# Matmul diagonal with softmax: reading half of the partitions in another block order

## The chip, the core and the metric

The kernel runs on one core of a Trainium2 chip. The metric is the device time of one execution in microseconds (us). Four of the core's engines have work here: VectorE (DVE in the profile) multiplies and sums, ScalarE (ACT) copies, sums some rows and takes exponentials, SyncE (SP) issues nearly all transfers, and sixteen DMA engines move the data between HBM and SBUF, the on-chip memory of 128 partitions. TensorE is not used.

## What is computed

```python
B, N, D = 8, 4096, 512          # x, y: float32
gram = np.matmul(x, y.transpose(0, 2, 1))
diag = np.diagonal(gram, axis1=1, axis2=2)
diag = diag - diag.max(axis=-1, keepdims=True)
exp = np.exp(diag)
return (exp / exp.sum(axis=-1, keepdims=True)).astype(np.float32)
```

Only the diagonal of the product is wanted, so each output needs one dot product of a row of x with the same row of y: 8 x 4096 dot products of length 512, then a softmax over the 4096 values of each batch. Each input has 67.1 MB and is read once; the output has 0.13 MB.

## The kernel before

**Tiling.** The eight batches are two sets of four (`Q`). In a set, a batch has 32 partitions (`G`), and each partition has 128 consecutive rows (`C`) of the batch, that is 128 x 512 x 4 B = 256 KB one after the other in HBM. Partition p of a set thus begins 256 KB behind partition p - 1, over all 128 partitions. A step `t` takes 32 of the 128 rows (`R`) of every partition: 64 KB a partition from x and 64 KB from y. There are eight steps (`S`): 0 to 3 for the first set, 4 to 7 for the second. `columns(t, r0, n)` gives the place of a step's rows among the 128, and with it the columns of `diag[set]` (128 partitions x 128) that receive the dot products.

**Buffers.** There are two tiles for x (`xs`, steps alternate) and one for y (`ys`). `xflat` and `yflat` are the same memory seen as 128 x 16384 elements (and some more).

**A step of the loop (lines 132 to 143).** SyncE issues one load of x (L70, helper `load_x`) and one of y (L73, `load_y`), 8 MB each, in this order over all steps. ScalarE copies the last 6 rows of y to `side` (L135). VectorE multiplies x by y in place, 26 rows from `ys` and 6 rows from `side` (L77), so that `ys` is free after the first of the two. It then sums 30 rows (L80), and ScalarE sums the other 2 (L85). The load of y for step t + 1 has to wait until the first product of step t has read `ys`; the load of x for step t + 2 has to wait until the sums of step t have read their tile. The x of step t + 1 has been issued before that, so it is what the queue works on during the products of step t.

**Softmax of the first set.** After step 3 `exps` takes the maximum of `diag[0]` along the columns (L105), then over the 32 partitions of a batch (L99), and the exponential with its sum (L112). `normalize` (L116 to L119) follows in step 4 and leaves the result in `res[0]`. It is not stored at once.

**The end.** Step 6 has other shares between VectorE and ScalarE. Step 7 is loaded in eleven pieces (lines 163 to 184) and worked off row by row with a fused multiply and sum (L88). Behind the last load, the one of L184, SyncE issues the stores of `res[0]` (L191) in six pieces: four of 16 partitions and two of 32. Then the softmax of the second set runs, and ScalarE issues the store of `res[1]` (L193).

**Order and waits of transfers.** Everything SyncE issues goes through one queue in the order of the program. A transfer signals its end on one of eight semaphores, which are taken in turn; a transfer whose semaphore is still in use by the one eight places earlier waits for that one.

Of the kernel before, what the change touches and what calls it, by code (L numbers as in the profile page):

```python
# [11 lines left out]
def kernel(  # L12
# [6 lines left out]
    nc = tc.nc  # L19
# [5 lines left out]
    B, N, D = x.shape  # L25
    P = nc.NUM_PARTITIONS
    G = 32
    Q = P // G
    C = N // G
    R = 32  # L30
    H = R // 2
# [10 lines left out]
    xv = x.rearrange("(s b) (j c) d -> s (b j) c d", b=Q, j=G)  # L42
    yv = y.rearrange("(s b) (j c) d -> s (b j) c d", b=Q, j=G)
    ov = out.rearrange("(s b) (j c) -> s (b j) c", b=Q, j=G)
# [5 lines left out]
    xflat = [big.tile([P, R * D + E], f32, name=f"xs{i}") for i in range(2)]  # L50
    yflat = big.tile([P, R * D + E], f32, name="ys")
    xs = [t[:, : R * D].rearrange("p (r d) -> p r d", d=D) for t in xflat]
    ys = yflat[:, : R * D].rearrange("p (r d) -> p r d", d=D)
# [3 lines left out]
    res = [small.tile([P, C], f32, name=f"res{i}") for i in range(B // Q)]  # L57

    def columns(t, r0, n):
        c0 = t % (C // R) * R + r0  # L60
        return slice(c0, c0 + n)

    def rows(t, r0, n):
        return xs[t % 2][:, r0 : r0 + n, :]

    def dots_of(t, r0, n):
        return diag[t * R // C][:, columns(t, r0, n)]

    def load_x(t, r0, n):
        nc.sync.dma_start(out=rows(t, r0, n), in_=xv[t * R // C, :, columns(t, r0, n), :])  # L70

    def load_y(t, r0, n):
        nc.sync.dma_start(out=ys[:, r0 : r0 + n, :], in_=yv[t * R // C, :, columns(t, r0, n), :])  # L73

    def products(t, r0, n, yt):
        xt = rows(t, r0, n)
# [30 lines left out]
    def exps(i, d):  # L107
        mxp = small.tile([P, 1], f32, name=f"mxp{i}")
        largest(mxp, d)
        nmx = over_quadrant(f"nmx{i}", mxp, Alu.max, negate=True)  # L110
        sump = small.tile([P, 1], f32, name=f"sump{i}")
        nc.scalar.activation(out=res[i], in_=diag[i][:, :C], func=Act.Exp, bias=nmx, scale=1.0, accum_out=sump)  # L112
        return sump

    def normalize(i, sump):
        total = over_quadrant(f"sum{i}", sump, Alu.add)  # L116
        rc = small.tile([P, 1], f32, name=f"rc{i}")
        nc.vector.reciprocal(out=rc, in_=total)  # L118
        nc.vector.tensor_single_scalar(out=res[i], in_=res[i], scalar=rc, op=Alu.mult)  # L119
# [12 lines left out]
    for t in range(S - 2):  # L132
        load_x(t, 0, R)
        load_y(t, 0, R)
        nc.scalar.activation(out=side, in_=ys[:, R - K :, :], func=Act.Copy)  # L135
        if t == C // R:
            normalize(0, sump)
        products(t, 0, R - K, ys[:, : R - K, :])
        products(t, R - K, K, side)
        sums(t, 0, R - W)  # L140
        sums_act(t, R - W, W)
        if t == C // R - 1:
            sump = exps(0, diag[0])

    t = S - 2
    load_x(t, 0, R)
    load_y(t, 0, R)
    spare = rows(t + 1, R - L, L)
    nc.scalar.activation(out=spare, in_=ys[:, F - L : F, :], func=Act.Copy)  # L149
# [13 lines left out]
    for load, n in (  # L163
        (load_x, H - 1), (load_y, F), (load_x, 8), (load_y, 9), (load_x, 6), (load_y, 3), (load_y, 1)
    ):
        load(t, upto[load], n)
        upto[load] += n
        both = min(upto.values())
        dots(t, done, both - done)
        done = both  # L170
        if done == F:
            largest(diag[1][:, C : C + 1], diag[1][:, C - 2 * R : C - R + H])

    first = (R - 3) * D
# [12 lines left out]
    met = small.tile([P, C - R], f32, name="met")  # L187
    nc.scalar.activation(out=met, in_=diag[1][:, : C - R], func=Act.Copy)  # L188

    for p, n in ((0, H), (H, H), (2 * H, H), (3 * H, H), (4 * H, 2 * H), (6 * H, 2 * H)):  # L190
        nc.sync.dma_start(out=ov[0, p : p + n, :], in_=res[0][p : p + n, :])  # L191
    normalize(1, exps(1, diag[1][:, C - R + H :]))
    nc.scalar.dma_start(out=ov[1], in_=res[1])  # L193

# [29 lines left out]
```

## Time and profile before

| | |
|---|---|
| median of 3 runs | 320.05 us (319.78 to 320.19) |
| the profiled execution | 319.75 us |
| its span, first to last instruction | 318.0 us |
| VectorE busy | 241.7 us (76%) |
| ScalarE busy | 49.9 us (16%) |
| read from HBM, mean rate over the span | 134.22 MB, 423 GB/s |
| y of step 0 lands | 42.15 us |
| last piece of x lands | 313.20 us |

The page shows one profiled execution. Engine rows give the busy time, the share of the span and the number of instructions. The DMA digits show, in 40 equal slices, the mean busy share of the 16 DMA engines in tenths, with 9 for 90% or more. A DMA packet is the piece of a transfer that one DMA engine moves at a time; here a packet of a big load is one partition's 64 KB. The chain of waits goes back from the last instruction to what released it, step by step, so it shows which work set the end. "SPq" is SyncE's queue, "ACTq" that of ScalarE.

### The profile page before, as it was taken

How to read it: one execution, taken by the hardware profiler on the slowest of the kernel's cores; microseconds unless marked ns; L12 is line 12 of the kernel's file. 1: busy time of each engine (PE TensorE's matmuls, PEld its weight loads, DVE VectorE, ACT ScalarE, POOL GpSimd, SP SyncE). 2: the span in 40 equal slices, each digit the busy share in tenths (PEclk: the TensorE clock that was granted, in tenths of full speed). 3: DMA queues.
4: the chain of work that ended last, by engine and by line, in shares of the span. 5: the costliest groups of instructions: out<-in, count | busy, mean ns of one | idle time of the engine just before them, and what ended most of it. 6: DMA issues, size and time to landing. Idle time of an engine off the chain costs nothing.

```text
span 318.0 us, 320 instructions
## 1 busy us (share of the span) xinstructions
DVE 241.7 (76%) x101; ACT 49.9 (16%) x97; POOL 0.2 (0%) x4
## 2 busy tenths in 40 slices
DVE  0000069995899939999399995999939998599995
ACT  1000030100301003010020103101030100596700
POOL 0000000000000000000000000000000000000000
DMA  9999999999999999999999999999999999999993
GB/s 381 412 396 486 437 396 437 478 404 396 486 437 396 445 478 396 396 486 437 396 470 453 396 396 511 412 396 478 445 396 412 495 412 396 433 439 404 442 410 131
DMA packets 3970, 134.37 MB, mean 423 GB/s; under 512 B 512, under 2 KB 896, under 8 KB 1536
## 3 DMA queue, kind: packets, MB, share of 16 engines
q1 hardware_dynamic: 3824, 134.29, 97.9%
q10 hardware_dynamic: 144, 0.07, 0.1%
q14 instruction: 2, 0.02, 0.0%
HBM read 134.22 MB, written 0.13 MB: 423 GB/s over the span
## 4 chain that ended last, share of the span: by engine, by line
DMA 70%; DVE 28%; issue 0%; SPq 0%; ACT 0%; DVEq 0%
DMA ys<-in_y_dram 59%; DVE xs L77 28%; DMA xs<-in_x_dram 11%; DVE xs L88 0%; SPq L73 0%; SPq L70 0%; DVE res L119 0%; DVE sum L99 0%; DVE nmx L99 0%; ACT res L112 0%; DVE mxp L105 0%; DVE rc L118 0%; DVEq L77 0%; DVEq L88 0%; SPq L130 0%
## 5 line engine op out<-in xcount | busy, mean ns | idle before, releaser
L77 DVE TENSOR_TENSOR xs<-xs,ys 128x13312 f32<-128x13312 f32 (+2 forms) x8 | 96.7, 12091 | 69.9 <-DMA ys<-in_y_dram 69.9
L80 DVE TENSOR_REDUCE diag<-xs 128x30 f32<-128x15360 f32 (+1 forms) x7 | 98.1, 14019 | 0.2
L85 ACT ACTIVATE xs<-xs 128x512 f32<-128x512 f32 x42 | 25.9, 618 | 90.4 <-DVE xs L77 90.4
L135 ACT ACTIVATE side<-ys 128x3072 f32<-128x3072 f32 x6 | 16.6, 2765 | 124.0 <-DMA ys<-in_y_dram 124.0
L88 DVE SCALAR_TENSOR_TENSOR xs<-xs,ys 128x512 f32<-128x512 f32 (+2 forms) x33 | 20.0, 673 | 0.8 <-DMA ys<-in_y_dram 0.7
L77 DVE TENSOR_TENSOR xs<-xs,side 128x3072 f32<-128x3072 f32 x6 | 20.1, 3351 | 0.0
L85 ACT ACTIVATION_READ_ACCUMULATOR xs<-xs 128x1 f32 x42 | 7.9, 188 | 0.0
L149 ACT ACTIVATE xs<-ys 128x4608 f32<-128x4608 f32 x1 | 4.0, 4045 | 19.9 <-DMA ys<-in_y_dram 19.9
L112 ACT ACTIVATE res<-diag,nmx 128x128 f32<-128x128 f32 x2 | 0.8, 403 | 29.8 <-DVE nmx L99 29.8
L77 DVE TENSOR_TENSOR xs<-xs,xs 128x4608 f32<-128x4608 f32 x1 | 5.0, 4951 | 0.0
L88 DVE DVE_READ_ACCUMULATOR xs<-xs,ys 128x1 f32 x33 | 2.8, 84 | 0.0
L123 ACT ACT_TABLE_LOAD x1 | 1.3, 1283 | 0.7 <-PEq L208 0.7
L99 DVE TRANSPOSE_TENSOR_REDUCE sum<-sump 128x1 f32<-128x32 f32 x2 | 0.4, 211 | 1.2 <-ACT res L112 1.2
L127 DVE MEMSET ys<- 128x1 f32 x1 | 0.1, 59 | 1.4 <-PEq L208 1.4
L119 DVE TENSOR_SCALAR res<-res,rc 128x128 f32<-128x128 f32 x2 | 0.6, 286 | 0.1
L105 DVE TENSOR_REDUCE mxp<-diag 128x1 f32<-128x128 f32 (+1 forms) x2 | 0.5, 228 | 0.1
L99 DVE TRANSPOSE_TENSOR_REDUCE nmx<-mxp 128x1 f32<-128x32 f32 x2 | 0.4, 211 | 0.1
L105 DVE TENSOR_REDUCE diag<-diag 128x1 f32<-128x64 f32 (+1 forms) x2 | 0.4, 204 | 0.0
L118 DVE RECIPROCAL rc<-sum 128x1 f32<-128x1 f32 x2 | 0.3, 162 | 0.1
L112 ACT ACTIVATION_READ_ACCUMULATOR res<-diag,nmx 128x1 f32 x2 | 0.4, 188 | 0.0
L188 ACT ACTIVATE met<-diag 128x96 f32<-128x96 f32 x1 | 0.3, 284 | 0.0
L208 POOL MEMSET const-bfloat16-1.0<- 128x1 bf16 x1 | 0.1, 101 | 0.0
(3 smaller groups left out, 0.3 us busy)
## 6 DMA issues: line engine op xcount, KB each, us to landing
ys<-in_y_dram SPq DMA_DIRECT2D x1, 4352.0 KB, 14.8
xs<-in_x_dram SPq DMA_DIRECT2D x1, 3840.0 KB, 14.1
ys<-in_y_dram SPq DMA_DIRECT2D x1, 2304.0 KB, 12.2
xs<-in_x_dram SPq DMA_DIRECT2D x1, 2048.0 KB, 19.3
xs<-in_x_dram SPq DMA_DIRECT2D x1, 1536.0 KB, 15.6
ys<-in_y_dram SPq DMA_DIRECT2D x1, 768.0 KB, 16.9
ys<-in_y_dram SPq DMA_DIRECT2D x3, 256.0 KB, 18.2
xs<-in_x_dram SPq DMA_DIRECT2D x1, 608.0 KB, 18.1
```

What stands on the lines that cost most here:

```text
L77: nc.vector.tensor_tensor(out=xt, in0=xt, in1=yt, op=Alu.mult)
L80: nc.vector.tensor_reduce(out=dots_of(t, r0, n), in_=rows(t, r0, n), axis=X, op=Alu.add)
L85: nc.scalar.activation(out=row, in_=row, func=Act.Copy, accum_out=dots_of(t, r, 1))
L88: nc.vector.scalar_tensor_tensor(out=xt, in0=xt, scalar=1.0, in1=yt, op0=Alu.mult, op1=Alu.mult, accum_out=out)
L99: nc.vector.tensor_reduce(out=got, in_=column.to_broadcast([P, G]), axis=X, op=op, negate=negate, apply_transpose=True)
L105: nc.vector.tensor_reduce(out=out, in_=d, axis=X, op=Alu.max)
L112: nc.scalar.activation(out=res[i], in_=diag[i][:, :C], func=Act.Exp, bias=nmx, scale=1.0, accum_out=sump)
L118: nc.vector.reciprocal(out=rc, in_=total)
L119: nc.vector.tensor_single_scalar(out=res[i], in_=res[i], scalar=rc, op=Alu.mult)
L123: nc.scalar.preload_act_table(Act.Exp)
L135: nc.scalar.activation(out=side, in_=ys[:, R - K :, :], func=Act.Copy)
L149: nc.scalar.activation(out=spare, in_=ys[:, F - L : F, :], func=Act.Copy)
```

## The change

The loads of steps 0 to 3 get a new source. For partitions 0 to 63 it is block t of 32 rows as before; for partitions 64 to 127 it is block t ^ 2, so 2, 3, 0, 1 over the four steps. Both halves are still one transfer: its source is a pattern written out by hand that counts 2 halves, then 64 partitions, then the 64 KB. The destination is the flat view of the tile, 128 partitions by 64 KB. From step 4 on the source is what it was, written flat.

The columns of `diag[0]` stay those of step t for all partitions, so in partitions 64 to 127 the columns 0 to 63 and 64 to 127 have changed places. The store of the first set puts this right: it goes in eight pieces of 16 partitions, and each row is stored as two halves of 64 elements (256 B), which are exchanged where p is 64 or more.

```diff
+    def source(a, t, r0, n):
+        if t >= C // R:
+            return (xv if a is x else yv)[t * R // C, :, columns(t, r0, n), :].rearrange("p c d -> p (c d)")
+        lower, upper = t * R * D, (t ^ 2) * R * D
+        return bass.AP(
+            a.tensor, lower + r0 * D, [[Q // 2 * N * D + upper - lower, 2], [C * D, P // 2], [1, n * D]]
+        )
+
     def load_x(t, r0, n):
-        nc.sync.dma_start(out=rows(t, r0, n), in_=xv[t * R // C, :, columns(t, r0, n), :])
+        nc.sync.dma_start(out=xflat[t % 2][:, r0 * D : (r0 + n) * D], in_=source(x, t, r0, n))
 
     def load_y(t, r0, n):
-        nc.sync.dma_start(out=ys[:, r0 : r0 + n, :], in_=yv[t * R // C, :, columns(t, r0, n), :])
+        nc.sync.dma_start(out=yflat[:, r0 * D : (r0 + n) * D], in_=source(y, t, r0, n))
...
-    for p, n in ((0, H), (H, H), (2 * H, H), (3 * H, H), (4 * H, 2 * H), (6 * H, 2 * H)):
-        nc.sync.dma_start(out=ov[0, p : p + n, :], in_=res[0][p : p + n, :])
+    for p in range(0, P, H):
+        first, second = (0, C // 2) if p < P // 2 else (C // 2, 0)
+        nc.sync.dma_start(
+            out=bass.AP(out.tensor, p * C + first, [[C, H], [second - first, 2], [1, C // 2]]),
+            in_=res[0][p : p + H, :].rearrange("p (u c) -> p u c", u=2),
+        )
```

## The prediction

> **What bounds the kernel now.** I read the busy slices and queue table of the page first, then the table by stretches, then the chain of waits, then SyncE's own waits at the tail.
>
> The page, busy share of the 16 DMA engines in 40 slices, then packets:
>
> ```profile
> DMA  9999999999999999999999999999999999999993
> ...
> DMA packets 3970, 134.37 MB, mean 423 GB/s; under 512 B 512, under 2 KB 896, under 8 KB 1536
> ...
> q1 hardware_dynamic: 3824, 134.29, 97.9%
> q10 hardware_dynamic: 144, 0.07, 0.1%
> ```
>
> The loads fill the DMA engines from end to end; VectorE is busy for 76% only. The packet counts show how a transfer is dealt out. SyncE's queue has 25 loads of 128 rows (3200 packets), 128 stored rows of 512 B, and 31 transfers; 3824 - 3200 - 128 = 496 = 31 x 16. ScalarE's queue: 144 = 128 + 16. So each transfer ends in 16 completion packets, and the 32 x 16 = 512 of them are all the packets under 512 B. A store of 16 rows has 16 as a load of 128 has.
>
> Stretches of the trace: from:to, length, busy us by engine, clock, DMA share, GB/s:
>
> ```profile
> 3.00:42.20 39.20, 0.00 (x0) 0.02 (x1) 0.00 (x0) 1.00 0.99 430
> ...
> 56.30:95.00 38.70, 33.43 (x4) 4.11 (x5) 0.00 (x0) 1.00 1.00 434
> 95.00:133.65 38.65, 33.47 (x4) 4.10 (x5) 0.00 (x0) 1.00 1.00 434
> ```
>
> A step's 16.78 MB go at 434 GB/s with all 16 engines busy, 27.1 GB/s each. The packet records of the trace say the same: a 64 KB row takes 2.418 us on its engine, the quickest of 1792 takes 2.415. HBM holds nothing back there; each engine is at its own pace.
>
> The chain of waits (start, length, what):
>
> ```profile
> 1.28 40.87 DMA ys<-in_y_dram
> ...
> 42.25 14.04 DVE xs L77
> 56.29 0.02 SPq L73
> ...
> 95.00 0.02 SPq L73
> ...
> 249.64 0.02 SPq L73
> ...
> 298.41 14.80 DMA xs<-in_x_dram
> ...
> 315.26 0.29 DVE res L119
> ```
>
> The 14.04 us of products look like compute on the path, but during them the queue still works off the next step's x (share 1.00 above). The period is that of the loads: (249.64 - 56.29) / 5 = 38.67 us a step, 19.33 us a load. Step 0 has 2.2 us more (40.87), for the first packets. The last x lands at 298.41 + 14.80 = 313.2, and 4.8 us of softmax and store follow.
>
> **The change part by part.** *Source order of steps 0 to 3.* The eight loads carry the same bytes in the same 128 rows of 64 KB. What is new is the shape: the source was one count of 128 rows, now it is a count of 2 (halves), then 64 rows, while the SBUF side stays 128. How that is dealt to the engines decides everything, and the trace of before has no such transfer. Bounds:
>
> - dealt as before over 16 engines: 128 / 16 x 2.418 = 19.3 us a load, nothing changes;
> - dealt by the first count on both sides: 2 shares, so 2 engines with 64 rows each, 64 x 2.418 = 154.8 us a load (or 8 x 19.33 = 154.7 from the chain).
>
> The nearest rows are the 32 transfers of before. First counts are 128, 32 and 16 on both sides, and each was cut in 16: the 8 KB stores into single rows. Every cut the trace shows can be a cut along the first count; none had to go along a second one. A first count of 2 offers two shares, and I take 2 engines.
>
> [...]
>
> Could one engine alone be quicker than among 16? The nearest packets are the 8 KB instruction fetches, six of them before any load: quickest of the eight 0.307 us, 26.7 GB/s. So no quicker; 2.418 us stands. From the other side, the median of those eight is 0.465 us: 0.16 us more of latency which a lone stream may fail to hide.
>
> Sum: a step of two loads goes from 38.67 to 8 x 38.67 = 309.4 us, +270.7. Four steps: +1082.8. Nothing in these steps can fill the gap, nor stretch it: products (14.04 us) lie beside the next x load (now 155 us), sums likewise, and load_y(t+1) still queues while x(t+1) runs, so the two engines never run dry. Step 4's x is dealt over 16 again; engines 2 to 15 take their shares early, yet engines 0 and 1 do theirs only after step 3's y, so steps 4 to 7 keep their length. Span 318.0 + 1082.8 = 1400.8.
>
> *Issue.* An issue of L70 or L73 takes 0.33 to 0.55 us now; a source with one dimension more may cost the spread of these, 0.2 us. All but step 0's lie under a running load. On the path once: 0 to +0.2 us, taken as 0. Without the cover it would be eight times that.
>
> *Exchange of columns.* In `diag[0]` the upper partitions' columns 0 to 63 and 64 to 127 change places. Maximum, exponential and sum run over whole rows, so no instruction changes: 0, either way.
>
> *Eight stores for six.* They are issued behind the last loads:
>
> ```profile
> SPq L191 <- DMA ys<-in_y_dram: 7.2, 4, 5.1
> SPq L191 <- DMA xs<-in_x_dram: 4.4, 2, 3.3
> ```
>
> Each store waits for a load, in the order in which a transfer eight places earlier finishes (eight completion semaphores, 64 increments each, in the trace). Stores 1 to 6 wait for y, x, y, y, x, y, as in these rows; the last now goes out at 312.1. Store 7 would wait for the last row of y, store 8 for the last x at 313.2. It is issued until 313.6 and lands, at the 2.1 us of the quickest present store, about 315.7. ScalarE's store of the second set is issued at 315.57 and takes 1.6 us, to 317.2. So 1.5 us of cover: 0. Pieces of 256 B twice as many: 512 B rows take 0.027 us each, 256 x 0.027 / 16 = 0.4 us at most, under that cover. Gone cover would cost what exceeds it, up to 1 us if landing takes 4.1 us (the median). No engine waits behind the stores on SyncE's queue but the end of the program.
>
> Total: span 1400.8. The profiled execution took 319.75 us for a span of 318.0, 1.75 around it: 1402.5. The median of the runs shown, 320.05, lies 0.3 higher: **1403 us**.
>
> **Rivals.**
>
> *A. Sixteen engines as before, not slower.* If the cut follows the SBUF side's 128 partitions, whatever the source's count, each load keeps 19.33 us and the time is 320.0. For it: the dealing of before fits the SBUF rows just as well, since they equal the source's. Against it: an engine's share would then have to start in the middle of a count of the source. It decides for the whole change, at the first load. Chance 0.13, with 319.5 to 320.4.
>
> *B. Sixteen engines, and HBM answers better.* The halves now read 128 KB apart from the common 256 KB pitch. To win is what slow packets lose: the first 16 rows take 2.4 to 3.1 us, 0.48 us above 2.418 on the mean, once; after that there is nothing (1.00 share, 434 GB/s). That alone gives 319.5, no change by what can be told; for more the remainder of step 0's 2.2 us would have to go too, 317.9. Chance of that 0.02. [...]
>
> *C. Sixteen engines, but the tail is late.* Store 8 lands after ScalarE's store: up to +1 us, 321. It begins to cost above 1.5 us of delay. Chance 0.02.
>
> **How the numbers follow.** Two engines 0.83: all 32 transfers fit a cut by the first count, and none shows the other kind; A is left its 0.13 because those 32 can't separate source from destination. Within the first case the low end is 1390 (2.415 us a packet gives 1401, and some us less if steps overlap better at their ends), the high end 1480 (512 packets on each engine x 0.16 us of latency = 81 us more). I hold 0.97 of that case inside, 0.80 of all. About 0.2%, 0.64 us, is what a measurement of this kernel can tell from no change. Slower 0.83 + 0.02 = 0.85, same 0.13 (A), faster 0.02 (B).
>
> **What would show it.** Right: DMA digits of 1 over some 35 of the 40 slices (2 of 16 busy), about 54 GB/s, then 9; the first wait of L77 for y until about 313 us (42.15 + 270.7); a period of L73 of 309 us in steps 1 to 3, 38.7 after; completions of the eight loads down to 2, so SyncE's queue at 3824 + 128 + 32 - 8 x 14 = 3872 packets. Sixteen engines would show 3984 packets and 434 GB/s. The dealing rests on no row of its own; if digits of 9 stand in the first slices, that step was wrong and the rest of the sum with it. A digit of 1 with a period far from 309 us would put the fault in the pace of an engine alone.

## The result

The changed kernel takes 1423.97 us (median of 6, 1423.4 to 1424.31), the one before 319.91 us in the same session: 4.45 times as long, 95% interval 4.4456 to 4.4545. The forecast was 1403 us with a range of 1390 to 1480. The profiled execution has a span of 1422.5 us where the sum gave 1400.8.

The page of the changed kernel, busy share of the DMA engines in 40 slices and packets:

```profile
DMA  1111111111111111111111111119211111129998
...
DMA packets 3954, 134.37 MB, mean 94 GB/s; under 512 B 560, under 2 KB 880, under 8 KB 1520
...
q1 hardware_dynamic: 3808, 134.28, 23.5%
q10 hardware_dynamic: 144, 0.07, 0.0%
```

A digit of 1 is 2 of 16 engines, and it stands as long as the new loads run, but for the 9 and the 2 that cover 960 to 1031 us (see below). The completions count them too. There are 34 transfers now. With 16 completions each, but 2 for the eight new loads, there would be 34 x 16 - 8 x 14 = 432; the packets under 512 B are 560, and 560 - 432 = 128 are the 256 B halves of the 64 exchanged rows.

Stretches of the changed kernel (from:to, length, busy us by engine, clock, DMA share, GB/s):

```profile
2.00:312.00 310.00, 0.00 (x0) 0.01 (x1) 0.00 (x0) 1.00 0.13 54
...
966.00:1005.00 39.00, 0.00 (x0) 0.00 (x0) 0.00 (x0) 1.00 0.95 198
1020.00:1240.00 220.00, 0.00 (x0) 0.00 (x0) 0.00 (x0) 1.00 0.13 54
1280.00:1380.00 100.00, 84.44 (x13) 10.39 (x13) 0.00 (x0) 1.00 0.98 420
```

0.13 is 2 / 16, and 54 GB/s is twice the 27.1 GB/s of one engine: the two engines run at the pace they had among sixteen. The second line is odd. There the share is 0.95, yet the rate is less than half of the 434 GB/s that such a share gave before.

The chain of waits (start, length, what). A load that completes on two engines only has no name here, so the y loads of steps 0 to 3 stand as an unknown queue:

```profile
1.39 311.33 another core or an unknown queue
...
346.31 275.58 another core or an unknown queue
...
655.47 275.42 another core or an unknown queue
...
964.46 296.64 another core or an unknown queue
...
1275.28 24.80 DMA ys<-in_y_dram
...
1402.87 14.78 DMA xs<-in_x_dram
...
1419.70 0.29 DVE res L127
```

The y loads land at 312.72, 621.89, 930.89 and 1261.10: periods of 309.2, 309.0 and 330.2 us. The first two are the forecast's 309.4. The third is 21 us longer, nearly the whole difference between 1400.8 and 1422.5. The stretch with the odd rate lies in it: there the x load of step 4, issued at 964.5, runs on engines 2 to 15 beside step 3's x on engines 0 and 1. The packet records show 64 KB rows of 4.4 to 5.2 us on all sixteen engines from 966 to 1007 us of the span, and 2.42 us before and after. By the landings it is step 3's x alone that is late: it takes 175.8 us (930.9 to 1106.7), where the x loads of steps 1 and 2 took 154.8 and 154.6; step 3's y takes 154.4 us like the y loads before it. (The records don't name an engine, but since one row follows the other without a gap, they show which rows share one: in the slow stretch two engines go on with step 3's x and fourteen have 8 rows each of step 4's. Of the 16 completions of step 4's x, 14 come by 1007.2 us and 2 at 1280.4. The two are called engines 0 and 1 here, the fourteen engines 2 to 15.)

### The profile page after: what moved, and what is told of

It is laid out like the page before. It is cut to its first block, busy times and chain, and to the rows that moved or that the text cites. A ratio compares the mean times of both kernels' runs of the same rounds, so it can differ in the third digit from the quotient of the medians.

```text
span 1422.5 us, 322 instructions
## 1 busy us (share of the span) xinstructions
DVE 241.7 (17%) x101; ACT 49.8 (3%) x97; POOL 0.2 (0%) x4
## 3 DMA queue, kind: packets, MB, share of 16 engines
q1 hardware_dynamic: 3808, 134.28, 23.5%
## 4 chain that ended last, share of the span: by engine, by line
another core or an unknown queue 81%; DVE 10%; DMA 8%; issue 0%; SPq 0%; ACT 0%; DVEq 0%
DVE xs L85 7%; DMA ys<-in_y_dram 5%; DVE diag L88 3%; DMA xs<-in_x_dram 2%; DVE xs L96 0%; SPq L81 0%; DVE res L127 0%; DVE sum L107 0%; DVE nmx L107 0%; ACT res L120 0%; DVE mxp L113 0%; DVE rc L126 0%; DVEq L85 0%; DVE ys L135 0%
```

## The experiments

Two questions were open: what sets the number of engines, and what took 21 us.

**First count of 4, 16, 32 and 64.** The source of the loads in steps 0 to 3 gets `k` groups, each 4 rows further on than the one before (4 rows back in steps 2 and 3); the stores are those of before. The edit against the changed kernel's `source`, shown with 16:

```diff
-        lower, upper = t * R * D, (t ^ 2) * R * D
+        k, shift = 16, 4 * D if t < 2 else -4 * D
         return bass.AP(
-            a.tensor, lower + r0 * D, [[Q // 2 * N * D + upper - lower, 2], [C * D, P // 2], [1, n * D]]
+            a.tensor, (t * R + r0) * D, [[P // k * C * D + shift, k], [C * D, P // k], [1, n * D]]
         )
```

> The loads of steps 0 to 3 have a source whose first count is 4 (four groups of 32 partitions, each 4 rows further on than the one before), the stores are those of before; the rows that steps 0 to 3 read are thus not all those of the reference. If the first count of the source sets the number of DMA engines: 4 engines, 32 rows each, 32 x 2.418 us = 77.4 us a load, 154.7 us a step, span 318.0 + 4 x (154.7 - 38.67) = 782 us, up to 10 us more where the load of step 4 runs beside step 3's. Rival, any source with three dimensions is slow: about 1422 us as with a first count of 2. Rival, the cut follows the SBUF side: 318 us (which the changed kernel's 1422.5 already speaks against).

> As the one with 4, but 16 groups of 8 partitions: a first count of 16. If the first count sets the number of engines: 16 engines, 19.3 us a load, span 318 us, although the source has three dimensions. Rival, three dimensions are slow by themselves: far over 318 us. Rival, sixteen engines but dealt in another order than before, so that two engines write the same part of SBUF at a time: half the rate, 77 us a step, span 473 us.

> As the one with 16, but 64 groups of 2 partitions: a first count of 64 against 128 in SBUF. If the number of engines is the largest up to 16 that divides both first counts: 16 engines, span 318 us. Rival, the counts must be equal (128 and 128, 16 and 16) for 16 engines, or the dealing collides: 473 us or more.

> As with a first count of 16 (487 us, packets of 5 us), but 32 groups of 4 partitions. [...] Rival, the rate grows with the first count by itself: between 318 and 486 us.

Spans, of one run each: 1121.4 us with 4, 486.3 with 16, 318.9 with 32, 318.1 with 64. Stretches within steps 0 to 3, first with 4, then 16, then 32:

```profile
20.00:290.00 270.00, 0.00 (x0) 0.00 (x0) 0.00 (x0) 1.00 0.25 58
400.00:540.00 140.00, 0.00 (x0) 0.00 (x0) 0.00 (x0) 1.00 0.25 69
600.00:750.00 150.00, 0.00 (x0) 0.00 (x0) 0.00 (x0) 1.00 0.25 79
860.00:940.00 80.00, 0.00 (x0) 0.00 (x0) 0.00 (x0) 1.00 0.25 106
```

```profile
90.00:320.00 230.00, 94.97 (x9) 9.53 (x14) 0.00 (x0) 1.00 1.00 207
330.00:450.00 120.00, 105.71 (x16) 17.01 (x26) 0.00 (x0) 1.00 1.00 434
```

```profile
90.00:240.00 150.00, 130.34 (x18) 16.88 (x22) 0.00 (x0) 1.00 1.00 435
```

The share settles the engine count: 0.25 is 4 of 16, and 16, 32 and 64 give 1.00 (64 with 433 GB/s from 20 to 300 us). The source with 2 groups of 64 partitions got two engines, the one with 64 groups of 2 got sixteen, so it is the first count that sets the number, and a third dimension costs nothing by itself. No run has a first count that isn't a power of two, so whether it has to divide isn't shown. But the number of engines isn't all. With 16 groups every engine is busy and the rate is 207 GB/s, half of the 435 that 32 groups have in an otherwise equal kernel; its plain loads, after 330 us, are back at 434. The expectation for 4 (782 us) failed too: four engines at 27.1 GB/s would give 108, but they begin at 58 and creep up to 106.

The rival for 16 (473 us) comes near the 486.3 us, but its reason, two engines that write the same part of SBUF at a time, isn't shown: the rates don't tell which partitions an engine writes. What the place in SBUF does to the rate is tried with the loads alone, below. Why the rate with 4 creeps up from 58 to 106 GB/s isn't shown either.

**Halves as two transfers.** The exchange with plain sources of 64 partitions (in a helper for both inputs: `a` is x or y, and `out` is the stretch of its tile that the load fills; the loads from step 4 on stay as they were):

```diff
-        nc.sync.dma_start(out=xflat[t % 2][:, r0 * D : (r0 + n) * D], in_=source(x, t, r0, n))
+        for p, block in ((0, t), (P // 2, t ^ 2)):
+            nc.sync.dma_start(
+                out=out[p : p + P // 2],
+                in_=bass.AP(a.tensor, (p * C + block * R + r0) * D, [[C * D, P // 2], [1, n * D]]),
+            )
```

> The change's exchange, whole and with its stores, but each load of steps 0 to 3 as two transfers of 64 partitions with a plain source (first count 64). If only the dealing to two engines cost the time: 16 engines for every transfer, 8 x 2 loads of 9.7 us, 320 us, the same within 1 us; what better answers of HBM are worth would show as 0.5 us at most. Rival, a transfer into 64 partitions reaches SBUF at a lower rate than one into 128: up to half, 77 us a step in steps 0 to 3, 475 us.

489.88 us, 1.532 times before (1.5295 to 1.5346): the rival. Its stretch within steps 0 to 3:

```profile
90.00:320.00 230.00, 95.18 (x9) 9.53 (x14) 0.00 (x0) 1.00 0.99 205
```

All engines are busy at half the rate, as with 16 groups. The obvious repair of the change thus loses half the rate in steps 0 to 3 as well: 205 GB/s, where the plain loads into 128 partitions had 434. What holds a load into 64 partitions to this isn't shown.

**The exchange for odd partitions.** The same amount of data is moved to the other blocks, in a shape whose first count is 64 (the stores put even and odd rows back, not shown):

```diff
-            a.tensor, lower + r0 * D, [[Q // 2 * N * D + upper - lower, 2], [C * D, P // 2], [1, n * D]]
+            a.tensor, lower + r0 * D, [[2 * C * D, P // 2], [C * D + upper - lower, 2], [1, n * D]]
```

> The change with another half of the partitions: the odd ones take blocks 2, 3, 0, 1, so the source counts 64 pairs, then 2, then 64 KB; the stores put even and odd rows back in eight pieces. If the first count of 64 keeps sixteen engines and HBM holds nothing back: 320.0 us, within 0.2% of before. Rival, the exchange of blocks wins something in HBM once the engines are all used: 319.3 us or less. Rival, the eight finer stores show: up to 321 us.

320.31 us, 1.0016 times before (1.0007 to 1.0026): no gain from HBM, if anything a trace of loss. The chain of waits shows a place for it, the first wait for y, which in the kernel before read "1.28 40.87":

```profile
1.57 40.97 DMA ys<-in_y_dram
```

SyncE's issue of the first, finer x load takes longer (0.68 us for 0.39), so y starts 0.29 us later; behind that the periods are those of before.

**The stores alone.** Loads as before, eight stores in two halves a row.

```diff
-    for p, n in ((0, H), (H, H), (2 * H, H), (3 * H, H), (4 * H, 2 * H), (6 * H, 2 * H)):
-        nc.sync.dma_start(out=ov[0, p : p + n, :], in_=res[0][p : p + n, :])
+    for p in range(0, P, H):
+        nc.sync.dma_start(
+            out=bass.AP(out.tensor, p * C + C // 2, [[C, H], [-(C // 2), 2], [1, C // 2]]),
+            in_=res[0][p : p + H, :].rearrange("p (u c) -> p u c", u=2),
+        )
```

> The kernel before with the eight stores in two halves of 256 B a row alone, the halves exchanged in all rows; the loads are those of before, so the columns of the first set come out exchanged. If the stores lie under the 1.5 us until the store of the second set lands: 320.0 us, within 0.2% of before. Rival, the tail waits for store 8: up to 1 us more, 321 us.

320.17 us, 1.0009 times before (1.0 to 1.0018), span 318.0 as before: so the stores lie under the tail.

**Step 4's x held back.** A copy of one element on VectorE, from the tile that this load overwrites, makes it wait:

```diff
         products(t, 0, R - K, ys[:, : R - K, :])
+        if t == C // R - 1:
+            nc.vector.tensor_copy(out=hold, in_=xs[(t + 1) % 2][:, 0, :1])
```

> The changed kernel, but the x load of step 4 waits until step 3's first product has been taken (a one-element copy of its tile on VectorE), so that it no longer runs beside step 3's loads on two engines. If the 21 us by which step 3 was longer than steps 1 and 2 (330.2 against 309.1 us) came from that overlap: step 3's y lands near 1240 us instead of 1261, and the span is about 1422.5 - 21 + 14 + 2 = 1417 us, since x of step 4 now begins 14 us after that landing. If step 3 is longer by itself: y lands at 1261, span near 1438 us.

Span 1417.1 us. The chain:

```profile
964.56 275.58 another core or an unknown queue
...
1254.84 40.87 DMA ys<-in_y_dram
```

Step 3's wait is 275.58 us, as in the steps before it (296.64 in the changed kernel): its y lands at 1240.1. The 21 us came from the overlap. The kernel, run once, is even 5 us faster than the changed one, whose six runs have spans of 1421.6 to 1422.5 us, though it starts that load 290 us later.

**Step 4's x from one stretch of HBM.** It reads 8 MB without the 256 KB distances (two lines at the head of `source`).

```diff
+        if t == C // R and a is x:
+            return bass.AP(a.tensor, Q * N * D, [[R * D, P], [1, R * D]])
```

> The changed kernel, but the x load of step 4 reads 8 MB that lie one after the other in HBM (64 KB a partition behind the last, not 256 KB), so step 4 multiplies other rows than the reference. In the changed kernel the 64 KB packets took 5.1 us while this load ran beside step 3's x. If the 256 KB distance in HBM makes them slow: 2.4 us a packet now, step 3's y lands near 1240 us, span about 1402 us. If the cause is on the side of SBUF or the engines: packets of 5.1 us, step 3's y near 1261 us, span 1422 us.

Span 1422.2 us. Step 3's wait for y, and the stretch that answers to the odd one:

```profile
964.51 296.80 another core or an unknown queue
...
966.00:1005.00 39.00, 0.00 (x0) 0.00 (x0) 0.00 (x0) 1.00 0.93 192
```

Step 3's y lands at 1261.3 as in the changed kernel (1261.1), and the rate is as low, so the distance in HBM isn't the cause.

**Loads alone, by where two engines write.** Two kernels of nothing but loads; each stage begins when VectorE has read what the last one loaded (`finish`). `sixteen` is the 8 MB load of 128 partitions. `two(tile, p0, n)` is a load whose source has a first count of 2, into the n partitions from p0 on and the n behind them. The second kernel has 28, 60 and 92 for p0 and no last stage.

```python
sixteen()
finish()
for p0 in (0, 8):
    two(slow0, p0, 4)
    two(slow1, p0, 4)
    sixteen()
    finish()
two(slow0, 0, P // 2)
sixteen()
finish()
```

> Not the reference's computation: a kernel of loads alone, in four stages, each begun when the one before has landed; its output is zeros. 1: an 8 MB load of 128 partitions alone. 2: two loads of 2 x 4 partitions (two engines), into partitions 0 to 7, and the 8 MB load beside them. 3: the same with partitions 8 to 15. 4: a load of 2 x 64 partitions and the 8 MB load beside it. [...]

The first kernel's stages: alone; into 0 to 7; into 8 to 15; beside a load of 2 x 64 partitions (no ScalarE column here):

```profile
5.00:21.00 16.00, 0.00 (x0) 0.00 (x0) 1.00 1.06 459
30.00:44.00 14.00, 0.00 (x0) 0.00 (x0) 1.00 0.97 421
72.00:102.00 30.00, 0.00 (x0) 0.00 (x0) 1.00 1.00 208
134.00:147.00 13.00, 0.00 (x0) 0.00 (x0) 1.00 1.01 413
```

With the small loads into partitions 0 to 7 the rate is 421 GB/s. With the same loads into 8 to 15 everything falls to 208, and the packet records have about 5.0 us on all sixteen engines. The fourth stage didn't repeat that, though its loads have the shapes that ran side by side in the changed kernel: its records have 4.84 us on two engines and 2.42 on the rest, at 413 GB/s. There both loads begin together; in the changed kernel step 3's x had run for 34 us (930.9 to 964.5) before step 4's was issued, about 14 rows on each engine. The second kernel tries three more places:

> The kernel of loads alone again, its output zeros: after the 8 MB load by itself, three stages of two loads of 2 x 4 partitions beside the 8 MB load, into partitions 28 to 35, then 60 to 67, then 92 to 99. [...]

Its stages: alone; into 28 to 35; into 60 to 67; into 92 to 99:

```profile
5.00:21.00 16.00, 0.00 (x0) 0.00 (x0) 1.00 1.04 451
32.00:43.00 11.00, 0.00 (x0) 0.00 (x0) 1.00 0.93 375
90.00:122.00 32.00, 0.00 (x0) 0.00 (x0) 1.00 1.02 205
154.00:183.00 29.00, 0.00 (x0) 0.00 (x0) 1.00 1.00 206
```

(In short stretches the rate is rough, since a packet is counted as a whole.) Leaving out the first and last row of an engine, the records have 4.9 to 5.0 us on two engines and 2.4 to 2.7 on the others in the second stage, and 5.0 to 5.3 us on all sixteen in the third and fourth, until the two engines come to their share of the 8 MB load. So the small loads slow two engines to half in one place (28 to 35) and all sixteen in three (8 to 15, 60 to 67, 92 to 99). What tells these places apart isn't shown. (With the place in SBUF the small loads' place in HBM moves too. That the cause lies in SBUF and not in HBM is my estimate; it rests on the kernel with one stretch of HBM, whose rates stayed low, and on the 16 and 32 groups, whose rows lie nearly the same distances apart in HBM and come at half and at full rate. Each of these stages ran once.) The changed kernel lost half the rate on every engine beside step 4's x, as these three places did: in its 41 us engines 0 and 1 moved 8 rows each of step 3 where 17 would have gone, and 9 x 2.42 is about the 21 us.

## Why the prediction was right, and where it was off

The measured 1424 us lies in the range, 21 us above the forecast. The mechanism was right, but that the range held is partly luck: it reached up to 1480 us for a latency that didn't come, and the 21 us came from something that the prediction had put at nothing.

**Two engines.** Right: 0.13 of sixteen engines, 54 GB/s, 2 completions a load, and the runs with 4 and 64 show that it is the first count.

**The pace of an engine alone.** Right: 2.418 us a row, 309.0 to 309.2 us a step against 309.4. The extra latency that widened the range to 1480 didn't come: a lone engine's packets follow without gaps, 128 rows in 309.0 to 309.2 us.

**"Engines 2 to 15 take their shares early, yet engines 0 and 1 do theirs only after step 3's y, so steps 4 to 7 keep their length."** This is the step that was off, and with it the words that nothing could stretch these steps. The order was right, but I took the early share for free. It costs 20 us of step 3: in the kernel before, step 3's y landed at 158.20,

```profile
133.68 24.52 DMA ys<-in_y_dram
```

so the sum puts it at 158.20 + 1082.8 = 1241.0, and it landed at 1261.1, because beside step 4's x the rows took 4.4 to 5.2 us on all sixteen engines and not 2.42. Holding the load back took this away. Steps 4 to 6 then have 39.0 to 39.1 us instead of 38.67, another 1 us; with the load held back steps 5 and 6 have 38.6 to 38.7. So this goes with the early load too, though by what way wasn't tried.

**Issue.** Taken as 0 with a bound of 0.2. The first x load took 0.65 us to issue in the changed kernel and 0.68 in the one for odd partitions, where it had been 0.39, so the bound was slightly too low. Step 0's y still lands at 312.7 for a forecast of 313.

**Exchange of columns and stores.** Right at 0: the stores alone leave the span at 318.0. The packet count was off (3808 for 3872): the lower 64 rows are stored in their own order, so their halves are one run of 512 B and not two of 256.

**Rivals.** Sixteen engines (A) is out. B, HBM answering better, is out too: with a first count of 64 the exchange, there for the odd partitions, gives 1.0016. C's late stores never showed.

## What to carry to other kernels

In these loads a transfer's speed hung on the shape of its patterns, not only on its bytes: the first count of the source decided how many DMA engines took part (0.13 of sixteen with 2, 0.25 with 4), and with all sixteen busy 16 groups gave 207 GB/s and 32 gave 435. Changing a source's address for some partitions cost under 1 us when the pattern still counted many small groups of partitions (32 or 64 here), but half the rate with 16 groups, three quarters and more with 4, and seven eighths with 2. Read the DMA share and the GB/s together: here a low share (0.13) was missing engines, and a full share at half the rate (207 GB/s) was rows that took about 5 us and not 2.42.

## What the hardware showed that I had not expected

Small loads on two engines can hold up all sixteen: into partitions 8 to 15, 60 to 67 or 92 to 99 the 8 MB load beside them came at 205 to 208 GB/s in all, while into 28 to 35 only two engines were slow (375 GB/s) and into 0 to 7 the rate was 421. Why the place makes the difference stays open; the runs show that it does, not how.

SyncE's issue itself can be held. SyncE's timeline in the changed kernel (start, length):

```profile
2.10 150.82 SPq L78 DMA_DIRECT2D xs<-in_x_dram  x1
326.93 0.51 SPq L81 DMA_DIRECT2D ys<-in_y_dram  x1
346.38 110.84 SPq L78 DMA_DIRECT2D xs<-in_x_dram  x1
```

The same load in the kernel before:

```profile
1.75 0.55 SPq L70 DMA_DIRECT2D xs<-in_x_dram  x1
```

The third load's issue takes 150.82 us and ends 5 us before the first load has landed (158.3 us), where it took 0.55 us before. What it waits for isn't shown. It cost nothing, since the next load on that queue had to wait for step 0's product until 326.9 us.
